# Two-by-two block products in the feed-forward input of a decoder layer

## The chip, the cores and the metric

The kernel runs on one core of a Trainium2 chip. The core has TensorE (matrix products, PE in the profile, its weight loads PEld), VectorE (DVE), ScalarE (ACT), GpSimd (POOL) and SyncE (SP, which here only issues transfers). Each engine works through its own list of instructions in order and waits on semaphores for the others. The metric is device time in microseconds (us) for one execution. Times from a profile are those of one profiled execution.

## The reference

The program is one layer of a decoder for 256 tokens of width 1024: gated attention and a recurrent branch, cross attention to a memory, and a feed-forward part. Only the last one is touched by the change:

```python
hn = rmsnorm(h, norm_ffn_g[l])
gu = hn @ w_ffn_in[l]
h = h + (jax.nn.silu(gu[..., :FFN_HIDDEN]) * gu[..., FFN_HIDDEN:]) @ w_ffn_out[l]
return rmsnorm(h, final_norm_g)
```

FFN_HIDDEN is 2816. So w_ffn_in is 1024 by 5632 and w_ffn_out 2816 by 1024, all in float32. rmsnorm divides each token by its root mean square and multiplies by a gain per feature.

## The kernel before, in words

A float32 product is made of three products of a shorter format: each operand is split into a part "hi" (the value rounded to the short format) and "lo" (the remainder), and hi by hi, hi by lo and lo by hi are summed in PSUM (mm3t, L237).

All weights come in units of 128 x 2048 values (1 MB), in the order of the list ORDER, one transfer each. prep (L169) sends one unit for, lets ScalarE copy it to hi (L194, two pieces of 1024 columns), and lets VectorE (576 columns of each piece) and GpSimd (448 of each piece) subtract to get lo (L198). There are two buffers for raw units and three pairs of hi and lo; nxt (L205) keeps two units of lead. The order of TensorE's instructions is as written in the code; on the other engines a scheduler orders them by the written order and by what is ready.

The feed-forward has eleven groups j of 256 hidden units. A group's input weights are two units ("I", j, kh): kh is the half of the 1024 input features, and the 512 columns are 256 gate columns and 256 value columns. Its output weights are one unit ("O", j). The steps, with the lines of before:

- turn_h2 (L1059) transposes 128 tokens by 512 features of the residual on TensorE, multiplies by the gain on VectorE and splits into H2 on ScalarE and GpSimd. The root mean square of a token is not applied here: it is a factor of a whole row and is applied in the gate.
- ffn_in (L1104) multiplies one unit with 128 tokens: four blocks of 128 features, three matmuls each, 12 matmuls of 512 columns into the bank psi. A group takes 48.
- gate (L1086) makes silu of one half on ScalarE (fg) and multiplies with the other half on VectorE (fu).
- turn_hid (L1094) transposes the gated hidden values (hidT) and splits them.
- ffn_out (L1119) multiplies one output unit: 24 matmuls into four PSUM banks acc, which stay open over the whole feed-forward.

The loop (L1125) goes I(j,0), turn_hid(j-1), I(j,1), O(j-1); the last output units are woven into the tail. PSUM has four banks for psi and hidT (pool mm) and four for acc.

In the attention's output product before it (pso), the residual H is updated and the first three of the four turn_h2 stand between its parts.

## Time and profile before

| | us |
|---|---|
| median of 3 runs | 624.67 (624.52 to 625.46) |
| the profiled execution | 625.08 |
| its span, first to last instruction | 623.1 |
| TensorE busy | 615.1 |
| VectorE busy | 395.6 |
| ScalarE busy | 334.1 |
| GpSimd busy | 371.5 |

The feed-forward's first matmul starts at 431.1 us. A row of the timeline gives start, length, engine, line, operation, output<-input and count; rows of a window table give, after the window, the busy time of PE, PEld, DVE, ACT and POOL with their counts, the granted TensorE clock, the share of the transfer engines and GB/s. A row of a group gives count, then busy time and mean nanoseconds, then the idle time ahead of it and what ended that.

### The profile page before, as it was taken

The numbers are of one execution on the slowest core, as the hardware profiler recorded it, in microseconds if no ns is written. First come the engines' busy times: TensorE is split into PE (matmuls) and PEld (weight loads), VectorE is DVE, ScalarE is ACT, GpSimd is POOL, SyncE is SP. The second block draws the span as 40 slices with busy tenths as digits, with TensorE's granted clock in tenths as the row PEclk, the third lists the DMA queues.
The fourth block names the chain that finished last, engine by engine and source line by source line (L and its number), as shares of the span: only waits on it lengthen the run. The fifth ranks groups of instructions, "written<-read, shape, count | busy, mean of one in ns | idle before, by whom it ended". The sixth has DMA issues, their size and how long they took to land.

```text
span 623.1 us, 8546 instructions
## 1 busy us (share of the span) xinstructions
PE 615.1 (99%) x3153; PEld 513.7 (82%) x3153; DVE 395.6 (63%) x691; ACT 334.1 (54%) x550; POOL 371.5 (60%) x296
## 2 busy tenths in 40 slices
PE   8999999999999999999999999999999999999995
PEld 7888888888877877778888888888888888888884
DVE  7589888979776875748846456754444444444433
ACT  7785554234376866727547556644543344434432
POOL 3888744556544564356857876656655665566553
PEclk9999999999999999999999999999999999999999
DMA  8754553334433333545454544453354455455511
GB/s 346 288 197 149 203 202 136 136 135 147 191 137 135 136 136 136 203 174 191 145 213 189 187 176 178 143 196 135 136 180 175 187 202 184 177 184 198 204 68 68
DMA packets 16890, 107.53 MB, mean 173 GB/s; under 512 B 2000, under 2 KB 2640, under 8 KB 4560
## 3 DMA queue, kind: packets, MB, share of 16 engines
q1 hardware_dynamic: 16128, 106.14, 46.9%
q10 hardware_dynamic: 720, 0.84, 0.4%
q8 instruction: 25, 0.41, 0.3%
q14 instruction: 17, 0.14, 0.1%
HBM read 105.92 MB, written 1.05 MB: 172 GB/s over the span
## 4 chain that ended last, share of the span: by engine, by line
PE 98%; DVE 0%; POOL 0%; issue 0%; POOLq 0%; DVEq 0%
PE pst L238 13%; PE pst L240 13%; PE pst L239 13%; PE psf L259 7%; PE psi L238 6%; PE psi L240 6%; PE psi L239 6%; PE psf L260 4%; PE acc L240 3%; PE acc L238 3%; PE acc L239 3%; PE lp L613 2%; PE psg L514 1%; PE pso L238 1%; PE pso L240 1%; PE pso L239 1%
## 5 line engine op out<-in xcount | busy, mean ns | idle before, releaser
L198 POOL TENSOR_TENSOR lo<-raw,hi 128x448 fp32r<-128x448 f32 x172 | 272.0, 1597 | 181.4 <-ACT hi L194 178.4
L194 ACT ACTIVATE hi<-raw 128x1024 fp32r<-128x1024 f32 (+1 forms) x194 | 196.2, 1037 | 161.1 <-PE pst L240 58.2
L198 DVE TENSOR_TENSOR lo<-raw,hi 128x576 fp32r<-128x576 f32 (+2 forms) x194 | 197.8, 1024 | 127.9 <-ACT hi L194 126.1
L238 PE MATMUL pst<-hi,XX 128*128 128x512 f32 x224 | 90.4, 404 | 0.0
L240 PE MATMUL pst<-hi,XX 128*128 128x512 f32 x224 | 87.4, 390 | 0.0
L239 PE MATMUL pst<-lo,XX 128*128 128x512 f32 x224 | 87.3, 390 | 0.0
L238 PE MATMUL psi<-hi,H 128*128 128x512 f32 x176 | 69.6, 395 | 0.0
L240 PE MATMUL psi<-hi,H 128*128 128x512 f32 x176 | 68.7, 390 | 0.0
L239 PE MATMUL psi<-lo,H 128*128 128x512 f32 x176 | 68.5, 389 | 0.0
L240 PEld LDWEIGHTS pst<-hi,XX 128*128 128x128 f32 x224 | 42.0, 188 | 9.0
L238 PEld LDWEIGHTS pst<-hi,XX 128*128 128x128 f32 x224 | 42.1, 188 | 8.8 <-issue 0.7
L239 PEld LDWEIGHTS pst<-lo,XX 128*128 128x128 f32 x224 | 42.1, 188 | 7.9
L240 PEld LDWEIGHTS psi<-hi,H 128*128 128x128 f32 x176 | 33.0, 188 | 7.1
L239 PEld LDWEIGHTS psi<-lo,H 128*128 128x128 f32 x176 | 33.1, 188 | 6.6
L238 PEld LDWEIGHTS psi<-hi,H 128*128 128x128 f32 x176 | 33.1, 188 | 6.5
L238 PE MATMUL acc<-hi,hid 128*128 128x512 f32 x86 | 33.6, 390 | 0.0
L240 PE MATMUL acc<-hi,hid 128*128 128x512 f32 x86 | 33.5, 389 | 0.0
L239 PE MATMUL acc<-lo,hid 128*128 128x512 f32 x86 | 33.5, 389 | 0.0
L1091 DVE SCALAR_TENSOR_TENSOR fu<-psi,r_h,fg 128x256 f32<-128x256 f32 x22 | 10.6, 483 | 25.1 <-ACT fg L1089 25.1
L1089 ACT ACTIVATE fg<-psi,r_h 128x256 f32<-128x256 f32 x22 | 10.4, 475 | 29.1 <-PE psi L240 29.1
L259 PE MATMUL psf<-H,hi 128*128 128x512 f32 x64 | 22.8, 400 | 0.0
L259 PE MATMUL psf<-XX,hi 128*128 128x512 f32 x64 | 22.6, 396 | 0.0
(336 smaller groups left out, 1199.4 us busy)
## 6 DMA issues: line engine op xcount, KB each, us to landing
raw<-w SPq DMA_DIRECT2D x94, 1024.0 KB, 4.8
raw<-w SPq DMA_DIRECT2D x4, 512.0 KB, 6.5
raw<-w SPq DMA_DIRECT2D x4, 256.0 KB, 4.0
H<-xtok SPq DMA_DIRECT2D x1, 1024.0 KB, 9.6
mraw<-mT SPq DMA_DIRECT2D x1, 1024.0 KB, 4.9
xraw<-xT SPq DMA_DIRECT2D x1, 512.0 KB, 6.5
gfin<-gfin SPq DMA_DIRECT2D x1, 512.0 KB, 3.7
out<-H SPq DMA_DIRECT2D x2, 256.0 KB, 2.0
```

Of the source, the lines that this page charges most:

```text
L194: SC.activation(hi[:, a], raw[:, a], AF.Copy)
L198: eng.tensor_tensor(lo[:, b], raw[:, b], hi[:, b].bitcast(F32), op=ALU.subtract)
L238: PE.matmul(ps, xh, h, start=first, stop=False)
L239: PE.matmul(ps, xh, l, start=False, stop=False)
L240: PE.matmul(ps, xl, h, start=False, stop=last)
L259: PE.matmul(ps, w[0][:, k, a], X2[:, :, k], start=k == 0, stop=False)
L260: PE.matmul(ps[:, 0], w[1][:, k, a], X2[:, 0, k], start=False, stop=k == 7)
L514: PE.matmul(pss[c][t], z[:, k, t * 128:(t + 1) * 128], ws[c][0][:, k], start=z is Xh and k == 0, stop=False)
L613: PE.matmul(ps[:, j], KS[:, a0 + j], QQ[:, a0 + j], start=True, stop=True)
L1089: SC.activation(g, ps[:, 0:256], AF.Silu, scale=r)
L1091: V.scalar_tensor_tensor(u, ps[:, 256:512], r, g, op0=ALU.mult, op1=ALU.mult)
```

## The change

Six of the eleven groups are joined to three double groups, (2,3), (5,6) and (8,9). In a double group the tokens are two halves, the features two halves and the weights four units: block 11 is I(q,0), 21 is I(q,1), 12 is I(q+1,0), 22 is I(q+1,1). Each output (group by token half) is the sum of two block products, eight in all. Now they are formed from seven products of combined blocks, called P1 to P7: three with plain tokens (P1, P2, P4) and four with sums and differences of token blocks, which token_sums makes once (tile SS). Weight blocks are combined in place on VectorE, two combinations ahead of P6 and two ahead of P5; each of the seven blocks is then split to hi and lo. Four of the products add up in one bank (P1, P6, P5, P3); ScalarE keeps its value after P1, P6 and P5, and VectorE adds a kept value to another bank (whole), after which the gate runs on GpSimd. Groups 0, 1, 4, 7 and 10 stay as they were.

A product is 12 matmuls, as one ffn_in part is. The plan has 42 units to split (10 I, 21 P, 11 O), where there were 33.

With it go: the split in one piece (VectorE 1152 columns, GpSimd 896) from the third unit on; a fourth pair of split tiles (px) and three units of lead; the root mean square applied to H before the transposes (hn), as sums of tokens need it, and no more in the gate; the first three units' parts for the first 128 tokens ahead of the second token half's transposes.

```diff
+SEVEN = ("P1", "P2", "P6", "P7", "P5", "P3", "P4")
+    out = two(0) + two(1)
+    out += seven(2, P2=[0], P5=[1]) + two(4)
+    out += seven(5, P2=[2], P7=[3], P5=[4]) + two(7)
+    out += seven(8, P2=[5], P7=[6], P5=[7])
+    out += [("I", 10, 0), ("O", 8), ("I", 10, 1)]
+    return out + [("O", 9), ("O", 10)]
...
+        def halve(raw, n):
+            if n % 4 == 3:
+                hi, lo = px[:, 0:2048], px[:, 2048:4096]
...
+            pieces = 2 if n < 2 else 1
...
+                SC.activation(hi[:, a], raw[:, a], AF.Copy)
+                cut = (c + 1) * w - POOL_COLS // pieces
+                V.tensor_tensor(lo[:, c * w:cut], raw[:, c * w:cut], hi[:, c * w:cut].bitcast(F32), op=ALU.subtract)
+                G.tensor_tensor(lo[:, cut:a.stop], raw[:, cut:a.stop], hi[:, cut:a.stop].bitcast(F32),
+                                op=ALU.subtract)
...
+        def block(q, name):
...
+                    SY.dma_start(blk[key], A["w"][where[("I",) + c]])
...
+            if name == "P6":
+                V.tensor_tensor(blk["12"], blk["22"], blk["12"], op=ALU.subtract)
+                V.tensor_tensor(blk["11"], blk["12"], blk["11"], op=ALU.add)
+                return blk["11"]
+            if name == "P7":
+                return blk["12"]
+            if name == "P5":
+                V.tensor_tensor(blk["21"], blk["21"], blk["11"], op=ALU.subtract)
+                V.tensor_tensor(blk["11"], blk["22"], blk["11"], op=ALU.subtract)
+                return blk["11"]
+            return blk["22"] if name == "P3" else blk["21"]
...
-        def gate(o, t):
-            r, ps = two["r"][:, t:t + 1], psi.pop((o, t))
-            g = t2("fg", (128, 256))
-            SC.activation(g, ps[:, 0:256], AF.Silu, scale=r)
-            u = t2b("fu", (128, 256))
-            V.scalar_tensor_tensor(u, ps[:, 256:512], r, g, op0=ALU.mult, op1=ALU.mult)
+        def gate(o, t, eng=V):
+            ps = psi.pop((o, t))
+            g = t2b("fg", (128, 256))
+            SC.activation(g, ps[:, 0:256], AF.Silu)
+            u = t2("fu", (128, 256))
+            eng.tensor_tensor(u, ps[:, 256:512], g, op=ALU.mult)
...
+        def token_sums():
+            a11, a12, a21, a22 = (h2g[t, c] for t in range(2) for c in range(2))
+
+            def put(i, g):
+                SC.activation(SS[:, 0, i], g, AF.Copy)
+                G.tensor_tensor(SS[:, 1, i], g, SS[:, 0, i].bitcast(F32), op=ALU.subtract)
+
+            V.tensor_tensor(a22, a21, a22, op=ALU.add)
+            s2 = t2("s2", (128, 4, 128))
+            V.tensor_tensor(s2, a22, a11, op=ALU.subtract)
+            put(1, s2)
+            V.tensor_tensor(a21, a11, a21, op=ALU.subtract)
+            put(2, a21)
+            put(0, a22)
+            V.tensor_tensor(a12, a12, s2, op=ALU.subtract)
+            put(3, a12)
...
+        def keep(key, ps, home):
+            SC.activation(home, ps, AF.Copy)
+            kept[key] = home
+
+        def whole(q, t, ps, key, eng):
+            c = t2("fc")
+            V.tensor_tensor(c, ps, kept.pop(key), op=ALU.add)
+            psi[q, t] = c
+            gate(q, t, eng)
...
+        prep_u(3)
+        for n in range(3):
+            ffn_in(n, 0)
+        turn_h2(1, hn1)
+        ffn_in(0, 1)
+        prep_u(4)
+        token_sums()
+        ffn_in(1, 1)
...
+        for n in range(4, len(units) - 2):
+            prep_u(n + 3)
```

More of the change, by code (lines that the diff above doesn't have):

```diff
@@ L70, with ffn_plan, seven, two @@
 ORDER = plan()
+SEVEN = ("P1", "P2", "P6", "P7", "P5", "P3", "P4")
+def ffn_plan():
+    def seven(q, **after):
+        out = []
+        for p in SEVEN:
+            out.append(("P", q, p))
+            out += [("O", o) for o in after.get(p, ())]
+        return out
+    def two(j):
+        return [("I", j, 0), ("I", j, 1)]
+    out = two(0) + two(1)
[4 more added lines that the diff above has]
+    return out + [("O", 9), ("O", 10)]
+FFN_PLAN = ffn_plan()
 def lay(ws):
@@ L1051, in build @@
         at[0] += 4
-        gfin = big("B4", "gfin", (128, 1024))
+        gf = big("B4", "gf", (128, 2048))
+        gfin = gf[:, 0:1024]
         SY.dma_start(gfin, A["gfin"].to_broadcast([128, 1024]))
@@ L1055, in build @@
         h2h, h2l = H2[:, 0], H2[:, 1]
+        where = {u: i for i, u in enumerate(ORDER)}
+        px = big("P1", "px", (128, 4096), F32R)
+        made_u, pair, blk = [0], {}, {}
+        def halve(raw, n):
+            if n % 4 == 3:
+                hi, lo = px[:, 0:2048], px[:, 2048:4096]
+            else:
+                hi = wh.tile([128, 2048], F32R, name="hi", tag="hi")
+                lo = wl.tile([128, 2048], F32R, name="lo", tag="lo")
+            pieces = 2 if n < 2 else 1
+            w = 2048 // pieces
+            for c in range(pieces):
+                a = slice(c * w, (c + 1) * w)
+                SC.activation(hi[:, a], raw[:, a], AF.Copy)
[3 more added lines that the diff above has]
+                                op=ALU.subtract)
+            return hi, lo
@@ new lines, in block @@
+        def block(q, name):
+            if name == "P1":
+                blk.clear()
+                for key, tag, c in (("11", "B10", (q, 0)), ("21", "B11", (q, 1)),
+                                    ("22", "B12", (q + 1, 1)), ("12", "B6", (q + 1, 0))):
+                    blk[key] = big(tag, "b" + key, (128, 2048))
+                    SY.dma_start(blk[key], A["w"][where[("I",) + c]])
+                return blk["11"]
+            if name == "P2":
+                return blk["21"]
+            if name == "P6":
[7 more added lines that the diff above has]
+                V.tensor_tensor(blk["11"], blk["22"], blk["11"], op=ALU.subtract)
+                return blk["11"]
+            return blk["22"] if name == "P3" else blk["21"]
@@ L1056, in wo_part, with prep_u @@
+        units = FFN_PLAN
+        def prep_u(upto):
+            while made_u[0] <= min(upto, len(units) - 1):
+                n = made_u[0]
+                made_u[0] += 1
+                u = units[n]
+                if u[0] == "P":
+                    raw = block(u[1], u[2])
+                else:
+                    raw = wr.tile([128, 2048], F32, name="raw", tag="raw")
+                    SY.dma_start(raw, A["w"][where[u]])
+                pair[n] = halve(raw, n)
         def wo_part(ps, t, c, kh):
@@ L1057, in wo_part @@
             t_part(ps, wo[2 * c + kh], (oxh, oxl), t, kh)
-        def turn_h2(t, c):
-            ks, ts = slice(4 * c, 4 * c + 4), slice(t * 128, (t + 1) * 128)
-            bk = bank("h2T", (128, 4, 128))
-            for j in range(4):
-                k = 4 * c + j
-                PE.transpose(bk[:, j], H[:, t, k * 128:(k + 1) * 128], ident)
-            g = t2("h2g", (128, 4, 128))
-            V.tensor_tensor(g, bk, bc(gv[:, V_FFN + 4 * c:V_FFN + 4 * c + 4], 128, 2), op=ALU.mult)
-            SC.activation(h2h[:, ks, ts], g, AF.Copy)
-            G.tensor_tensor(h2l[:, ks, ts], g, h2h[:, ks, ts].bitcast(F32), op=ALU.subtract)
@@ L1070, in build, with add_h2, rstd_h2 @@
-        todo = None
+        ssq2 = cp.tile([128, 4], F32, name="ssq2")
+        v2 = cp.tile([128, 2], F32, name="v2")
+        r2 = cp.tile([128, 2], F32, name="r2")
+        h2g = {}
+        def add_h2(t, c, ps):
+            d = H[:, t, c * 512:(c + 1) * 512]
+            V.tensor_tensor(d, ps, d, op=ALU.add)
+            SC.activation(t2b("hjunk"), d, AF.Square, scale=1.0 / 32.0, accum_out=ssq2[:, 2 * t + c:2 * t + c + 1])
+        def rstd_h2(t):
+            V.tensor_scalar(v2[:, t:t + 1], ssq2[:, 2 * t:2 * t + 1], ssq2[:, 2 * t + 1:2 * t + 2], EPS,
+                            op0=ALU.add, op1=ALU.add)
+            G.tensor_tensor(r2[:, t:t + 1], v2[:, t:t + 1], nhalf[:, :1], op=ALU.pow)
+            hn = []
+            for c in range(2):
+                n = t2("hn")
+                SC.activation(n, H[:, t, c * 512:(c + 1) * 512], AF.Copy, scale=r2[:, t:t + 1])
+                hn.append(n)
+            return hn
@@ new lines, in turn_h2 @@
+        def turn_h2(t, hn):
+            for c in range(2):
+                ks, ts = slice(4 * c, 4 * c + 4), slice(t * 128, (t + 1) * 128)
+                bk = bank("h2T", (128, 4, 128))
+                for j in range(4):
+                    PE.transpose(bk[:, j], hn[c][:, j * 128:(j + 1) * 128], ident)
+                g = t2("h2g", (128, 4, 128))
+                V.tensor_tensor(g, bk, bc(gv[:, V_FFN + 4 * c:V_FFN + 4 * c + 4], 128, 2), op=ALU.mult)
+                SC.activation(h2h[:, ks, ts], g, AF.Copy)
+                G.tensor_tensor(h2l[:, ks, ts], g, h2h[:, ks, ts].bitcast(F32), op=ALU.subtract)
+                h2g[t, c] = g
@@ L1071, in build @@
+        hn0 = None
         for t in range(2):
@@ L1074, in build @@
                 wo_part(ps, t, c, 0)
-                if todo:
-                    turn_h2(*todo)
+                if (t, c) == (1, 1):
+                    turn_h2(0, hn0)
                 wo_part(ps, t, c, 1)
-                add_h(t, c, ps, None, ssq2)
-                todo = (t, c)
-        ring = ("B7", "B14", "B10", "B11", "B12", "B6")
-        X2 = (h2h, h2l)
-        hid, acc, two, psi, hm = {}, {}, {}, {}, {}
-        def gate(o, t):
-            r, ps = two["r"][:, t:t + 1], psi.pop((o, t))
-            g = t2("fg", (128, 256))
-            SC.activation(g, ps[:, 0:256], AF.Silu, scale=r)
-            u = t2b("fu", (128, 256))
-            V.scalar_tensor_tensor(u, ps[:, 256:512], r, g, op0=ALU.mult, op1=ALU.mult)
+                add_h2(t, c, ps)
+            if t == 0:
+                hn0 = rstd_h2(0)
+        hn1 = rstd_h2(1)
+        hids = [big(tag, "hids", (128, 2, 2, 2, 256), F32R) for tag in ("B7", "B14")]
+        X2 = (h2h, h2l)
+        hid, acc, psi, hm = {}, {}, {}, {}
+        def gate(o, t, eng=V):
[4 more added lines that the diff above has]
+            eng.tensor_tensor(u, ps[:, 256:512], g, op=ALU.mult)
             hm[o, t] = u
@@ L1099, in turn_hid @@
                     PE.transpose(bk[:, j, t * 128:(t + 1) * 128], u[:, j * 128:(j + 1) * 128], ident)
-            hd = big(ring[o % 6], "hid", (128, 2, 2, 256), F32R)
+            hd = hids[o // 2 % 2][:, o % 2]
             split(bk, hd[:, 0], hd[:, 1])
             hid[o] = hd
-        def ffn_in(o, kh, t, w):
-            if kh == 0:
-                psi[o, t] = mm.tile([128, 512], F32, name="psi", tag="mm")
-            t_part(psi[o, t], w, X2, t, kh)
         def out_part(o, w, t, c, home=None, u=0, v=512):
@@ L1117, in out_part, with ffn_in @@
                      (o == 0 or home is not None) and k == 0, k == 1 and o >= NF // 2 - (2 if t and c else 1))
-        def ffn_out(o):
-            w = by_k(nxt(), 2)
+        def ffn_in(n, t):
+            _, o, kh = units[n]
+            if kh == 0:
+                psi[o, t] = mm.tile([128, 512], F32, name="psi", tag="mm")
+            t_part(psi[o, t], by_k(pair[n], 4), X2, t, kh)
+            if kh == 1:
+                gate(o, t)
+        SS = big("P0", "SS", (128, 2, 4, 4, 128), F32R)
@@ new lines, in tokens, with product @@
+        def tokens(name):
+            if name in ("P1", "P2", "P4"):
+                t, kh = {"P1": (0, 0), "P2": (0, 1), "P4": (1, 1)}[name]
+                return [[z[:, 4 * kh + k, t * 128:(t + 1) * 128] for k in range(4)] for z in X2]
+            i = {"P5": 0, "P6": 1, "P7": 2, "P3": 3}[name]
+            return [[SS[:, z, i, k] for k in range(4)] for z in range(2)]
+        def product(ps, name, w, first):
+            xh, xl = tokens(name)
+            for k in range(4):
+                for i, (x, z) in enumerate(((xh, w[0]), (xh, w[1]), (xl, w[0]))):
+                    PE.matmul(ps, x[k], z[:, k], start=first and k == 0 and i == 0, stop=k == 3 and i == 2,
+                              skip_group_check=not first)
@@ new lines, in build, with ffn_product @@
+        bank_of, kept = {}, {}
+        def keep(key, ps, home):
[6 more added lines that the diff above has]
+            gate(q, t, eng)
+        def ffn_product(n):
+            _, q, name = units[n]
+            w = by_k(pair[n], 4)
+            key = {"P1": "A", "P6": "A", "P5": "A", "P3": "A", "P2": "B", "P7": "F", "P4": "F"}[name]
+            first = name in ("P1", "P2", "P7")
+            if first:
+                bank_of[key] = mm.tile([128, 512], F32, name="pq" + key, tag="mm")
+            ps = bank_of[key]
+            product(ps, name, w, first)
+            if name == "P1":
+                keep("1", ps, t2("f1"))
+            elif name == "P2":
+                whole(q, 0, ps, "1", G)
+            elif name == "P6":
+                keep("2", ps, gf[:, 1024:1536])
+            elif name == "P5":
+                keep("4", ps, gf[:, 1536:2048])
+                whole(q + 1, 1, bank_of["F"], "4", G)
+            elif name == "P3":
+                psi[q + 1, 0] = ps
+                gate(q + 1, 0)
+            elif name == "P4":
+                whole(q, 1, ps, "2", G)
@@ L1121, in ffn_out @@
+        def ffn_out(n):
+            w = by_k(pair[n], 2)
             for t in range(2):
                 for c in range(2):
-                    out_part(o, w, t, c)
-        for u in ORDER[at[0]:-2]:
-            if u[0] == "O":
-                ffn_out(u[1])
-                continue
-            _, o, kh = u
-            w = by_k(nxt(), 4)
-            for t in range(2):
-                ffn_in(o, kh, t, w)
-                if (o, kh, t) == (0, 0, 0):
-                    turn_h2(1, 1)
-                    two["r"] = rstd2(ssq2, "h2")
-                if kh == 1:
-                    gate(o, t)
-            if kh == 0 and o:
-                turn_hid(o - 1)
+                    out_part(units[n][1], w, t, c)
@@ new lines, in build @@
+        prep_u(3)
[6 more added lines that the diff above has]
+        ffn_in(1, 1)
+        prep_u(5)
+        ffn_in(2, 1)
+        turn_hid(0)
+        prep_u(6)
+        for t in range(2):
+            ffn_in(3, t)
+        to_turn = [1]
+        for n in range(4, len(units) - 2):
+            prep_u(n + 3)
+            u = units[n]
+            if u[0] == "I":
+                for t in range(2):
+                    ffn_in(n, t)
+            elif u[0] == "P":
+                ffn_product(n)
+            else:
+                ffn_out(n)
+            if u[0] != "O" and u[2] in (0, "P1"):
+                for o in to_turn:
+                    turn_hid(o)
+                to_turn = []
+            if u[0] == "I" and u[2] == 1:
+                to_turn = [u[1]]
+            elif u[0] == "P" and u[2] == "P4":
+                to_turn = [u[1], u[1] + 1]
@@ L1143, in build @@
         n = NF // 2 - 1
-        wa = by_k(nxt(), 2)
-        wb = by_k(nxt(), 2)
+        wa, wb = (by_k(pair[len(units) - 2 + i], 2) for i in range(2))
         out_part(n - 1, wa, 0, 0)
@@ L1159, in build @@
         ssq3 = cp.tile([128, 5], F32, name="ssq3")
-        hg3 = {i: big(ring[j], "hg3", (128, 512)) for j, i in enumerate(((0, 0), (0, 1), (1, 0)))}
+        hg3 = {i: big(tag, "hg3", (128, 512)) for tag, i in zip(("B10", "B11", "B12"), ((0, 0), (0, 1), (1, 0)))}
         v3 = cp.tile([128, 3], F32, name="v3")
```

## The prediction

> **What bounds the kernel now.** I read the page first: engines, then the slices, then the costliest groups.

> ```profile
> PE 615.1 (99%) x3153; PEld 513.7 (82%) x3153; DVE 395.6 (63%) x691; ACT 334.1 (54%) x550; POOL 371.5 (60%) x296
> L198 POOL TENSOR_TENSOR lo<-raw,hi 128x448 fp32r<-128x448 f32 x172 | 272.0, 1597 | 181.4 <-ACT hi L194 178.4
> ```

> TensorE is busy throughout and never waits after the first microseconds, so fewer matmuls mean less time as long as it still never waits. The matmul "mean ns" of 390 overlaps its neighbours; what one costs is the distance of two starts. From the timeline of TensorE, then the table by stage for one feed-forward turn (two input units, one output unit) and for the whole feed-forward, and the chain:

> ```profile
> 595.72 0.39 PE L238 MATMUL psi<-hi,H 128*128 128x512 f32 x1
> ...
> 598.89 0.39 PE L240 MATMUL psi<-hi,H 128*128 128x512 f32 x1
> 447.90:464.70 16.80, 16.80 (x77) 13.90 (x76) 7.68 (x9) 7.35 (x9) 10.03 (x6) 1.00 0.53 188
> 430.00:600.00 170.00, 170.00 (x772) 140.73 (x771) 76.14 (x91) 74.52 (x93) 101.77 (x63) 1.00 0.50 181
> 448.10 0.44 PE hidT L1099 x4
> 464.89 0.44 PE hidT L1099 x4
> ```

> The two rows of the fence's top are 14 matmuls apart: 3.17 / 14 = 0.226 us a matmul. Twelve (one block product) take 2.72 us, a unit of 24 takes 5.44 us, and a turn of 72 with its transposes (0.47) the 16.79 us between the two hidT rows. In that turn GpSimd is busy 10.0 us and VectorE 7.7, for three weight units to split. That is slack now; the change splits a weight block per 2.72 us of TensorE, so the question is what a split costs.

> **What a split costs.** One unit's split in the timeline of VectorE and GpSimd, then a turn in which another VectorE instruction came between:

> ```profile
> 477.44 0.76 DVE L198 TENSOR_TENSOR lo<-raw,hi 128x576 fp32r<-128x576 f32 x1 [2.74 <-ACT hi L194]
> 478.39 1.43 DVE L198 TENSOR_TENSOR lo<-raw,hi 128x576 fp32r<-128x576 f32 x1 [0.19 <-ACT hi L194]
> 477.48 3.35 POOL L198 TENSOR_TENSOR lo<-raw,hi 128x448 fp32r<-128x448 f32 x2 [1.77 <-ACT hi L194]
> 466.74 0.69 DVE L286 TENSOR_TENSOR hid<-hidT,hid 128x512 fp32r<-128x512 f32 x1
> 467.50 0.96 DVE L198 TENSOR_TENSOR lo<-raw,hi 128x576 fp32r<-128x576 f32 x1
> 466.11 3.37 POOL L198 TENSOR_TENSOR lo<-raw,hi 128x448 fp32r<-128x448 f32 x2 [2.09 <-ACT hi L194]
> 476.34 2.01 ACT L194 ACTIVATE hi<-raw 128x1024 fp32r<-128x1024 f32 x2 [3.12 <-PE acc L240]
> ```

> The same VectorE instruction takes 0.76 us when it starts first and 1.43 when it starts in the middle of GpSimd's. It ends at 479.82; GpSimd's first of two pieces ends at the half of 3.35, at 479.16, and 0.66 us is left. So it stood still until GpSimd's instruction was over, and GpSimd's second piece then stood still for it: 4 turns, 0.66 + 1.01 + 0.66 + 1.01 = 3.35. An instruction of VectorE that reads two SBUF tiles and one of GpSimd exclude each other for their whole length. The hid row (one operand in PSUM) ran at its usual 0.69 beside GpSimd. I treat both engines' two-tile work as one queue, "the shared queue". Prices in it:

> ```profile
> L198 DVE TENSOR_TENSOR lo<-raw,hi 128x1024 fp32r<-128x1024 f32 x14 | 18.1, 1316 | 3.8 <-ACT hi L194 3.8
> 14.13 1.22 DVE L198 TENSOR_TENSOR lo<-raw,hi 128x1024 fp32r<-128x1024 f32 x1
> L198 DVE TENSOR_TENSOR lo<-raw,hi 128x512 fp32r<-128x512 f32 x8 | 5.4, 694 | 0.6 <-ACT hi L194 0.6
> 418.23 1.29 POOL L1068 TENSOR_TENSOR H<-h2g,H 128x512 fp32r<-128x512 f32 x1 [5.57 <-ACT H L1067]
> 387.02 0.74 POOL L973 TENSOR_TENSOR qxl<-kx,qxh 128x256 fp32r<-128x256 f32 x1 [1.82 <-ACT qxh L972]
> ```

> The new split is one piece each, 1152 and 896 columns: twice the pieces above less one fixed part (0.06), 1.27 + 1.96 = 3.23 us. A 2048-column combination is 2.2 (two of 1.22, each less some 0.1 of start). 512 columns cost 0.6 on VectorE and 1.17 on GpSimd, 256 on GpSimd 0.62: the rows less the 0.1 that lies outside the exclusion (0.76 against 0.66).

> **The change, part by part.** All sums are against the profiled execution (625.08 us, span 623.1); the median of the runs is 624.67, 0.4 lower.

> Matmuls: seven products of 12 instead of eight, three times: 36 x 0.2264 = 8.15 us less on the path. Transposes keep their number. That is the whole gain.

> Splits: 42 units (10 plain input, 21 products, 11 output) instead of 33. TensorE needs 63 x 2.72 + 11 x 0.47 = 176 us for them; the shared queue 42 x 3.23 = 136, 12 combinations 26, nine 256-column gate products now on GpSimd 6, token sums (4 of 0.6, 4 of 1.17) 7, the token transposes' two late remainders 2: 177. They are equal, so TensorE waits wherever the work bunches. I followed the changed program's engine queues, which are in order, with these prices.

> Transfers are the same megabytes. On SP's queue the four blocks of a group now wait for splits of the group before, and hold the next units behind them; landing takes 4.8 us (row below) and the nearest user comes some 10 us after the issue, so I cost this at nothing. What is queued behind a late block is VectorE's first combination, and behind that the gate that frees P3's bank: 4 us of slack.

> ```profile
> raw<-w SPq DMA_DIRECT2D x94, 1024.0 KB, 4.8
> L1066 DVE TENSOR_TENSOR h2g<-h2T,gv 128x512 f32<-128x512 f32 x4 | 2.8, 688 | 6.2 <-PE h2T L1064 6.2
> L1067 ACT ACTIVATE H<-h2g x4: 617/632/633, 417.5 to 435.2; 128x512 fp32r<-128x512 f32 x4
> ```

> Opening. The normed tokens must be whole before they are summed, so the second half turns only after three parts of 12. Its first psi part then waits for VectorE 0.69, ScalarE 0.63 and GpSimd: 1.9 us of TensorE idle before it. From there the shared queue holds, until the gate of unit (1, second tokens), which turn_hid(1) after P1 needs: two remainders 2.3, four sums 2.4, four sum remainders 4.7, three combinations 6.6, VectorE's part of P1, P2, O0 3.8, GpSimd's of P1, P2, O0, P6 7.8, and the gate 0.4: 28.0. TensorE has 16.8 in that stretch (three parts 8.16, turn 0.47, unit 5.44, P1 2.72). Stall 1.9 + 11.2 = 13.1, spread over the start and the turns of hidden 0 and 1. The floor is 2.6, if nothing excludes; the ceiling 18.7, with the GpSimd rows' 1.67 a piece (waits in them), 1.4 more for four.

> First double group to second. From there to GpSimd's gate product for P4, which turn_hid(2) needs: P6's VectorE part 1.3, eight splits (P7, P5, O1, P3, P4, I, I, P1) 25.8, GpSimd's part of the next P2 2.0, three combinations 6.6, three gates 1.9: 37.6. TensorE has P2, O0, P6, P7, P5, O1, P3, P4, I: 32.6. The stall is 4.6 to 5.0; I take 4.6 as the gate starts a little before. Then P1 waits 1.3 for a PSUM bank whose gate stands on VectorE behind a combination. Sum 5.9.

> Second to third: eleven splits 35.5, P2's two parts 3.2, four combinations 8.8, three gates 1.9: 49.4 against TensorE's 47.6. The bare difference is 1.8; three splits here (O2, P5, P3) come late, as ScalarE's copy (2.0, row above) waits for TensorE to free the pair or stands behind gates, and in my walk the queue is empty for some 3 us by that, of which half is lost. Stall 3.5, and the same 1.3: 4.8. For both later groups the floor is nothing, where the exclusion fails.

> Third to the end: no next group is prepared; O8 waits 1.9 for the hidden split behind O9's. The last output units and the tail are as before.

> Costed at nothing: ScalarE's copies (42 x 2.0 and some 40 small ones of 0.6 are 110 of about 195 us), the fourth pair of split tiles and the longer lead (they only let splits start earlier), the gate without its scale, the norm applied before the turn (four copies of 0.63, hidden by the three parts in front; it is what makes the opening wait).

> Sum: 13.1 + 5.9 + 4.8 + 1.9 - 8.15 = +17.5, so 642.6 as a profiled run and 642 as a median. Longer GpSimd pieces by a seventh (2.23 a block) bring it to 650, shorter by a tenth to 638.

> **The rivals.** *Faster.* The exclusion does not carry over to one long piece, or VectorE and GpSimd overlap; then of the stalls stay 2.6 at the opening and a few tenths, -8.15 + 2.8 = -5.3, 619. It decides where a split costs the shared queue less than about 2.7 us: group one then needs 32.6. Against it stands the 1.43 row, met in each turn I looked at. *Only the opening waits*, as later groups have some slack that I priced too tight: 13.1 - 8.15, 630. For it: between groups two and three the bare sums differ by 1.8 only. *The clock falls in the gaps.* TensorE has never been idle so far except at both ends:

> ```profile
> 1.56 3.57 PE L335 MATMUL warm<-still 128*128 128x256 f32 x15 [1.56 <-DVE still L332]
> 387.01 0.28 PE L238 MATMUL xs<-kxh,qxh 128*128 128x256 f32 x1
> 387.13 0.28 PE L239 MATMUL xs<-kxl,qxh 128*128 128x256 f32 x1
> 618.00:623.00 5.00, 0.00 (x0) 0.00 (x0) 0.91 (x3) 0.72 (x1) 0.55 (x1) 0.80 0.42 157
> ```

> The first fifteen matmuls run at 0.238 us each against 0.12 later, for 3.6 us: a cold start loses 1.8. A mean granted clock of 0.80 over the last 5 us, at half speed 2 of them, has it fall near 621, 4.4 us after the last matmul (about 616.6). My gaps are about 5.0, 3.9, 4.6 and 3.5 us. If all four lose 1.8 the time is 642 + 7 = 649; part is given back where the shared queue is late anyway. [...] *The change does not do what it says* is out: 36 matmuls fewer stand in the program.

> **How the numbers follow.** Main case, 636 to 645: 0.57. Clock as well, 646 to 651: 0.17. Only the opening, 628 to 635: 0.13. Faster, about 619: 0.11. Even, where both halves cancel: 0.02. The range 630 to 650 leaves out the faster case and a little at both ends. 0.2% (1.2 us) is about what a measurement here can tell: faster 0.11, same 0.02, slower 0.87.

> **What the profile would show.** Right: TensorE with some 25 us of idle in the feed-forward, before hidT of hidden 0 and 1, hidT of 2 and 5, released by VectorE or GpSimd gates; VectorE and GpSimd instructions there at two and three times their lone lengths (a split's VectorE part between 1.3 and 3.3, a combination 2.2 to 4.2); about 3117 matmuls. Wrong: splits side by side at 1.3 and 2.0 to 2.1 with TensorE unbroken, or gaps released by transfers. The largest risk is GpSimd's price for 896 columns, which no row shows in one piece.

## The result and the profile after

| | before | changed |
|---|---|---|
| median (us) | 625.07 (624.52 to 625.53) | 645.41 (644.99 to 645.98) |
| profiled execution, span (us) | 625.08, 623.1 | 644.99, 642.9 |

The ratio is 1.0326 (95% interval 1.0309 to 1.0344): the changed kernel is 20.3 us slower. The forecast was 642, range 630 to 650.

The first page of the changed kernel's profile, engines and slices (each digit the busy tenths of 16.1 us, PEclk the granted clock in tenths):

```profile
PE 614.4 (96%) x3117; PEld 510.3 (79%) x3117; DVE 457.5 (71%) x685; ACT 356.7 (55%) x545; POOL 424.7 (66%) x288
PE   8999999999999999999999999998889699799995
POOL 3888643665436643548768676555999879959843
PEclk9999999999999999999999999998899799999998
```

TensorE executes 36 matmuls less (3153 before) and yet is busy almost as long (615.1 before): part of its work, 10.1 us, ran at half clock (0.50 in the windows below). In slices 28 to 35 (434 to 563 us) it has holes, GpSimd is nearly full, and the clock row dips there too. What TensorE waited for in the feed-forward, from the table of waits (line, what it waited for: us in total, times, longest). Here hidT is the bank that turn_hid fills, and "hidden 2" below is its turn for group 2; pqA, pqB and pqF are the banks of the products:

```profile
PE hidT L1207 <- POOL fu L1199: 9.4, 3, 5.7
PE hidT L1207 <- DVE fu L1199: 4.8, 2, 2.5
PE psi L261 <- ACT H L1172: 2.8, 1, 2.8
PE pqA L1261 <- DVE hids L309: 0.9, 1, 0.9
PE acc L263 <- DVE hids L309: 0.8, 1, 0.8
PE psi L263 <- POOL H L1173: 0.8, 2, 0.4
PE acc L261 <- ACT hids L308: 0.5, 1, 0.5
```

20.0 us, 14.2 of them before the hidden turns (hidT) for a gate (fu). Before, there was no such wait at all. The table by stage, for 20 us without a hole in TensorE, and the timeline of GpSimd and VectorE there, show why the gates come late:

```profile
480.00:500.00 20.00, 20.00 (x90) 16.55 (x89) 19.08 (x10) 14.04 (x11) 20.00 (x7) 1.00 0.82 306
484.90 3.25 POOL L1099 TENSOR_TENSOR px<-b,px 128x896 fp32r<-128x896 f32 x1
488.11 3.25 POOL L1099 TENSOR_TENSOR lo<-b,hi 128x896 fp32r<-128x896 f32 x1
491.31 3.24 POOL L1099 TENSOR_TENSOR lo<-raw,hi 128x896 fp32r<-128x896 f32 x1
494.52 2.78 POOL L1199 TENSOR_TENSOR fu<-fc,fg 128x256 f32<-128x256 f32 x1
486.08 3.28 DVE L1098 TENSOR_TENSOR lo<-b,hi 128x1152 fp32r<-128x1152 f32 x1
489.89 2.67 DVE L1098 TENSOR_TENSOR lo<-raw,hi 128x1152 fp32r<-128x1152 f32 x1
493.11 3.60 DVE L1115 TENSOR_TENSOR b<-b,b 128x2048 f32<-128x2048 f32 x1 [0.54 <-DMA b<-w]
505.68 2.77 POOL L1199 TENSOR_TENSOR fu<-fc,fg 128x256 f32<-128x256 f32 x1
508.50 1.54 PE L1207 MATMUL hidT<-cst,fu 128*128 128x128 f32 x6 [5.66 <-POOL fu L1199]
```

GpSimd is busy for 20.00 of 20.00 us and starts a split every 3.21 us (484.90, 488.11, 491.31). A split must come every 2.72 us where TensorE runs one product after the other. VectorE's part of a split, 1.27 alone by the forecast, lies between 2.67 and 3.28 in these rows, and GpSimd's product of 256 columns takes 2.78, of which 0.62 was the forecast price alone: each stands still inside its row until the other engine's instruction is over (the VectorE row at 486.08 ends at 489.36, 1.21 us behind the end of GpSimd's row at 484.90). The lateness piles up until the gate that hidden 2 needs is over at 508.45, and TensorE has stood for 5.66 us.

### The profile page after: what moved, and what is told of

Same layout as the page of the kernel before. It is cut to its first block, busy times and chain, and to the rows that moved or that the text cites. A ratio compares the mean times of both kernels' runs of the same rounds, so it can differ in the third digit from the quotient of the medians.

```text
span 642.9 us, 8467 instructions
## 1 busy us (share of the span) xinstructions
PE 614.4 (96%) x3117; PEld 510.3 (79%) x3117; DVE 457.5 (71%) x685; ACT 356.7 (55%) x545; POOL 424.7 (66%) x288
## 4 chain that ended last, share of the span: by engine, by line
PE 75%; DVE 8%; POOL 6%; issue 4%; DMA 4%; ACT 3%; POOLq 0%; DVEq 0%; ACTq 0%
PE pst L261 13%; PE pst L263 12%; PE pst L262 12%; PE psf L282 7%; PE psf L283 4%; DVE lo L1098 3%; POOL lo L1099 3%; ACT hi L1096 2%; POOL px L1099 2%; PE pqA L1261 2%; PE lp L636 2%; DMA raw<-w 2%; PE acc L263 2%; DMA b<-w 1%; PE acc L261 1%
## 5 line engine op out<-in xcount | busy, mean ns | idle before, releaser
L221 POOL TENSOR_TENSOR lo<-raw,hi 128x448 fp32r<-128x448 f32 x106 | 161.9, 1541 | 111.4 <-ACT hi L217 108.5
L217 ACT ACTIVATE hi<-raw 128x1024 fp32r<-128x1024 f32 (+1 forms) x128 | 128.7, 1028 | 93.9 <-PE pst L263 58.1
L221 DVE TENSOR_TENSOR lo<-raw,hi 128x576 fp32r<-128x576 f32 (+2 forms) x128 | 130.1, 1024 | 58.3 <-ACT hi L217 57.1
L1099 POOL TENSOR_TENSOR lo<-raw,hi 128x896 fp32r<-128x896 f32 (+1 forms) x21 | 60.8, 2900 | 7.1 <-ACT hi L1096 6.0
L1099 POOL TENSOR_TENSOR lo<-b,hi 128x896 fp32r<-128x896 f32 x13 | 42.3, 3252 | 15.8 <-ACT hi L1096 13.8
L1098 DVE TENSOR_TENSOR lo<-raw,hi 128x1152 fp32r<-128x1152 f32 (+1 forms) x21 | 37.1, 1769 | 16.7 <-ACT hi L1096 16.6
L1096 ACT ACTIVATE hi<-raw 128x2048 fp32r<-128x2048 f32 (+1 forms) x21 | 36.5, 1748 | 11.7 <-DMA raw<-w 4.1
L263 PE MATMUL acc<-hi,hids 128*128 128x512 f32 x86 | 33.6, 391 | 0.8 <-DVE hids L309 0.8
L261 PE MATMUL acc<-hi,hids 128*128 128x512 f32 x86 | 33.7, 392 | 0.5 <-ACT hids L308 0.5
L261 PE MATMUL psi<-hi,H 128*128 128x512 f32 x64 | 26.3, 410 | 2.8 <-ACT H L1172 2.8
L1099 POOL TENSOR_TENSOR px<-b,px 128x896 fp32r<-128x896 f32 x8 | 27.6, 3449 | 1.4 <-ACT px L1096 1.3
L263 PE MATMUL psi<-hi,H 128*128 128x512 f32 x64 | 26.1, 407 | 0.8 <-POOL H L1173 0.8
L262 PE MATMUL psi<-lo,H 128*128 128x512 f32 x64 | 25.9, 405 | 0.0
## 6 DMA issues: line engine op xcount, KB each, us to landing
raw<-w SPq DMA_DIRECT2D x82, 1024.0 KB, 4.8
b<-w SPq DMA_DIRECT2D x12, 1024.0 KB, 5.4
H<-xtok SPq DMA_DIRECT2D x1, 1024.0 KB, 9.2
mraw<-mT SPq DMA_DIRECT2D x1, 1024.0 KB, 4.9
```

The costliest lines, as they stand in the source:

```text
L217: SC.activation(hi[:, a], raw[:, a], AF.Copy)
L221: eng.tensor_tensor(lo[:, b], raw[:, b], hi[:, b].bitcast(F32), op=ALU.subtract)
L261: PE.matmul(ps, xh, h, start=first, stop=False)
L262: PE.matmul(ps, xh, l, start=False, stop=False)
L263: PE.matmul(ps, xl, h, start=False, stop=last)
L1096: SC.activation(hi[:, a], raw[:, a], AF.Copy)
```

## The experiments

Two questions: is it the exclusion of VectorE and GpSimd (the shared queue) that costs the time, or the placing of the products, or the opening? And what does the clock add? In e1, e2 and e8 only the split of the 42 feed-forward units changes.

**e1: VectorE splits alone.**

```diff
+FFN_POOL = 0
-                cut = (c + 1) * w - POOL_COLS // pieces
+                cut = (c + 1) * w - FFN_POOL // pieces
```

GpSimd's instruction stands only where cut leaves it columns.

> The changed kernel, but VectorE makes the remainders of all 2048 columns in the feed-forward and GpSimd none (42 splits at 2.2 us on VectorE instead of 1.27 + 1.96). Shared queue (VectorE's two-tile work and GpSimd's exclude each other): 1.0 us less per split, 42 us less in that queue; the wait before the turn of hidden 2 falls from 5.7 to under 2, the one before hidden 5 goes, and about half of the opening's stays. 626 to 630 in all, GpSimd's lengths near their lone values. Rival, VectorE overloaded on its own (its 457 us busy are its own work, GpSimd is beside it): 0.9 us more per split on VectorE, the same waits or longer, 645 to 655. Rival, only the number of splits and the order of the lists matter: no change, 643 to 647.

Measured: 629.93 (629.31 to 630.04), ratio 1.0073 (1.0058 to 1.0088). A group of splits, then the waits:

```profile
L1099 DVE TENSOR_TENSOR lo<-b,hi 128x2048 fp32r<-128x2048 f32 x13 | 31.6, 2429 | 10.2 <-ACT hi L1097 10.2
PE hidT L1209 <- DVE fu L1201: 2.1, 1, 2.1
PE hidT L1209 <- POOL fu L1201: 1.7, 1, 1.7
```

One engine alone does all 2048 columns in 2.43 us, where two engines together needed 3.21. Giving one engine 44% of the columns made the pair slower than the other engine by itself. The waits before hidT fall from 14.2 to 3.8 us, and three quarters of the loss are gone (15.5 of 20.3 us).

**e2: half of GpSimd's share** (FFN_POOL = 448).

> The changed kernel with GpSimd's share of a feed-forward split halved, 448 of 2048 columns (VectorE 1600). Shared queue: a split costs 1.73 + 1.02 = 2.75 instead of 3.23, so the time lies between that of the change and that of the kernel without GpSimd's share, 629 to 634, and most of the gain is here already, as 2.75 is about what fits beside TensorE. Rival, the two engines overlap and the longer of both lists decides: VectorE 0.5 us longer a split, 645 to 650.

Measured: 633.85 (632.73 to 634.49), ratio 1.0132 (1.0115 to 1.0148), waits before hidT 6.5 us. By GpSimd's columns the time goes 629.9 (0), 633.9 (448), 645.4 (896): the second half costs three times the first, as one would expect of a queue that has some slack first and then none.

**e8: GpSimd as long at work, but only writing.** Two fills of its 896 columns take the place of the subtraction. It leaves out 7/16 of the remainders.

```diff
-                G.tensor_tensor(lo[:, cut:a.stop], raw[:, cut:a.stop], hi[:, cut:a.stop].bitcast(F32),
-                                op=ALU.subtract)
+                for _ in range(2):
+                    G.memset(lo[:, cut:a.stop].bitcast(F32), 0.0)
```

> The changed kernel; in place of its subtraction GpSimd fills its 896 columns of each feed-forward remainder with zeros, twice (so 7 of 16 of the weights' remainders are left out there). GpSimd keeps an instruction per split but reads no tile. If it is the reading of tiles by both that excludes: VectorE's parts stand at 1.3 us and its combinations at 2.2, the waits go as with VectorE alone, 620 to 630. If any instruction of GpSimd keeps VectorE out: VectorE's parts still at 2 to 3 us, and the time falls only by what the fill is shorter than the subtraction, 632 to 645.

Measured: 623.27 (622.66 to 623.43), ratio 0.9962 (0.9949 to 0.9975). From its timeline, a split of VectorE with GpSimd's fills:

```profile
486.35 1.36 DVE L1098 TENSOR_TENSOR lo<-raw,hi 128x1152 fp32r<-128x1152 f32 x1 [0.84 <-ACT hi L1096]
486.81 1.75 POOL L1100 MEMSET px<- 128x896 f32 x2 [0.96 <-PE pqA L1261]
```

The two run side by side at their lone lengths (1.36 is the length of a VectorE part that nothing disturbs). The eight VectorE parts that go from a block to px last 1.35 us in the mean here and 2.61 to 3.27 in the changed kernel, and the waits before hidT are down to one of 1.5 us. GpSimd is busy 1.75 us a unit, not far from the 1.96 that I had priced for its subtraction. So it is not that GpSimd works, and not that it writes; of what the runs varied, what is left is that both instructions read SBUF. VectorE's sum fc, with one input in PSUM, took 0.68 us beside GpSimd's subtraction in the changed kernel (at 489.29, in GpSimd's row at 488.11), and 0.68 to 0.69 in all six such sums. One thing this run does not hold constant: a fill needs no copy from ScalarE and so starts earlier. The lengths of the VectorE rows do not depend on that.

**e4: the gates on VectorE.** The product behind `whole` (three places) goes from GpSimd's full list to VectorE's.

```diff
-                whole(q, 0, ps, "1", G)
+                whole(q, 0, ps, "1", V)
```

> The changed kernel with the nine gate products on VectorE instead of GpSimd. The longest waits (hidden 2 and 5) ended with such a product on GpSimd. Shared queue: the product only moves to another place in the same queue, behind the same splits and combinations; 256 columns cost 0.33 instead of 0.62: 643 to 647. Rival, the product's place on GpSimd is the cause: 9.4 us of waits go, 635 to 638.

Measured: 649.61 (647.22 to 650.01), ratio 1.0382 (1.0362 to 1.0401); 2.6 us above the range that I expected, and the rival is out.

```profile
PE hidT L1207 <- DVE fu L1199: 15.5, 4, 5.5
```

The list in which the gate stands does not matter: its product waits for the same queue, now behind splits and combinations on VectorE. The waits in the feed-forward together are 20.3 us, as in the changed kernel; what the trace has more of is slow matmuls, 16.6 us of them at half clock (in three stretches of 6.83 us) against 10.1. No run separates the two.

**e10: the order alone.** The double groups are (3,4), (6,7) and (8,9), with other output units between them; GpSimd's share stays at 896.

```diff
-    out = two(0) + two(1)
-    out += seven(2, P2=[0], P5=[1]) + two(4)
-    out += seven(5, P2=[2], P7=[3], P5=[4]) + two(7)
+    out = two(0) + two(1) + [("I", 2, 0), ("O", 0), ("I", 2, 1)]
+    out += seven(3, P2=[1], P5=[2]) + two(5)
+    out += seven(6, P2=[3], P7=[4])
     out += seven(8, P2=[5], P7=[6], P5=[7])
-    out += [("I", 10, 0), ("O", 8), ("I", 10, 1)]
+    out += two(10) + [("O", 8)]
...
-            if u[0] != "O" and u[2] in (0, "P1"):
+            if u[0] != "O" and u[2] in (0, "P2" if u[1] == 8 else "P1"):
```

> The changed kernel with its splits and gates as they are (GpSimd 896 columns), and only the order of the kernel e9: the third plain group ahead of the first double group, the output units of e9. Shared queue: the opening's waits shrink, but each later group still asks 37 and more us of the queue in 33 of TensorE, so the work only meets later: 637 to 643. Rival, the crowded opening and the order are what cost the time and the share of GpSimd little: 624 to 630.

Measured: 643.82 (642.31 to 647.69), ratio 1.0313 (1.028 to 1.0347), 0.8 us above the range that I expected; its rival is out. The interval overlaps that of the changed kernel (1.0309 to 1.0344).

```profile
PE hidT L1207 <- POOL fu L1199: 12.3, 3, 6.4
PE pqF L1261 <- DVE fc L1272: 2.7, 1, 2.7
```

The waits move to other hidden turns and stay nearly as large (18.9 us in all for 20.0). With the queue full, spreading its work helps little or nothing.

**e3: the frame without products.** All units plain, no token sums; the norm ahead of the turn, the new opening and the one-piece splits stay.

```diff
-    out += seven(2, P2=[0], P5=[1]) + two(4)
-    out += seven(5, P2=[2], P7=[3], P5=[4]) + two(7)
-    out += seven(8, P2=[5], P7=[6], P5=[7])
+    for j in range(2, 10):
+        out += two(j) + [("O", j - 2)]
...
-        token_sums()
```

> The changed kernel's frame without its products: all eleven groups as plain units (33 splits), no token sums; the norm before the transposes, three parts for the first tokens ahead of the second turn, the fourth pair and the one-piece split stay. It has the matmuls of the kernel before. Shared queue: 33 x 3.23 = 107 us beside 180 of TensorE, so no wait but the opening's 1.9 + 0.8 before the first part for the second tokens: 627 to 629. Rival, the opening as such (new order, late norm) costs the 13 us that were put down to it: 636 to 640.

Measured: 630.78 (628.45 to 631.55), ratio 1.0082 (1.0061 to 1.0102), 2 us above what I expected. Its only waits in the feed-forward are those for the turned tokens:

```profile
PE psi L260 <- ACT H L1171: 2.2, 1, 2.2
PE psi L262 <- POOL H L1172: 1.0, 2, 0.6
```

That is 3.2 us; 3.4 us at half clock behind them (445.4 to 448.8, TensorE running throughout) lose 1.7 more. So the opening as such costs some 5 of the 5.7 us, and with 33 units to split, even in one piece each, no gate is late.

**e7: matmuls into two of the gaps**, to keep the clock up. 20 ahead of hidT of hidden 2 and 12 ahead of hidden 5, into a bank that is overwritten.

```diff
+            flat = bk.rearrange("p a b -> p (a b)")
+            for _ in range({2: 20, 5: 12}.get(o, 0)):
+                PE.matmul(flat, h2h[:, 0, 0:128], px[:, 0:512], start=True, stop=True)
```

> The changed kernel with matmuls whose result is overwritten ahead of the transposes of hidden 2 (20) and hidden 5 (12), 4.5 and 2.7 us of work in gaps of 5.7 and 3.5. The granted clock should stay full after the first of these gaps (it was half for 6.8 us from 505.3 on). If the half clock costs its full price, 3 us come back: 641 to 643. If the shared queue is late there anyway, TensorE only waits longer at the next turn (hidden 5): 644 to 646.

Measured: 645.48 (644.61 to 645.98), ratio 1.032 (1.0303 to 1.0338): nothing changed. Around hidden 2 the clock is full now, but in this run it is halved around hidden 1 (rows by windows: start:end, length, busy PE, PEld, DVE, ACT, POOL, clock, transfers):

```profile
505.30:512.10 6.80, 6.80 (x36) 5.67 (x35) 6.70 (x3) 2.92 (x3) 6.80 (x3) 1.00 0.08 34
465.09:468.50 3.41, 0.44 (x2) 0.20 (x2) 3.41 (x1) 0.52 (x1) 3.41 (x2) 1.00 0.21 29
468.50:471.91 3.41, 2.69 (x8) 2.21 (x9) 3.41 (x3) 1.96 (x2) 2.28 (x1) 0.50 0.67 279
```

TensorE ran for 9.5 us at half speed, with a third window from 444.6 on, against 10.1 in the changed kernel, so the run does not measure the clock's price. It is its rival (644 to 646) that came in. What the run does show: filling a gap shortens nothing when the gate is late for another reason. The waits fall to 12.9 us, and the 32 added matmuls are 32 x 0.2264 = 7.2: 20.1 again.

**b1: the kernel before with VectorE alone** splitting in the feed-forward, as a control.

```diff
+FFN_FIRST = ORDER.index(("I", 0, 0))
-                cut = (c + 1) * n - (0 if i in ALONE else POOL_COLS // pieces)
+                cut = (c + 1) * n - (0 if i in ALONE or i >= FFN_FIRST else POOL_COLS // pieces)
```

> The kernel before with VectorE making all of the remainders in the feed-forward, as a control: nothing waits for splits there (a 16.8 us turn has 10 us of them), so no change on either theory, 624.5 to 626; if the split by VectorE alone were faster in itself, the time would fall here too.

Measured: 625.17, ratio 1.0003 (0.9993 to 1.0012). The gain of e1 is not a gain that the kernel before could have had too: there the queue had slack.

**e9: VectorE alone and the order of e10 together**, splits in two pieces, the gates on VectorE.

```diff
+FFN_POOL = 0
-            pieces = 2 if n < 2 else 1
+            pieces = 2
...
-                whole(q, 0, ps, "1", G)
+                whole(q, 0, ps, "1", V)
```

The other two gates and the order of e10 likewise.

> The changed kernel with splits and gate products on VectorE alone (two pieces), and the double groups at (3,4), (6,7), (8,9) so that a third plain group stands ahead of the first one; output units placed after P2, P7 and P5, and O8 after the last input units. Shared queue: 7 of the 25 us of waits stood in the opening because token sums, three combinations and four splits met there; with 10.9 us more of TensorE's work ahead of them they go. Left are the wait for the second turn (1.9) and two or three of about 1 us: 8.15 - 5 = 3 less than before, 621 to 624. Rival, seven products cannot be fed in this kernel in any order: 628 to 632 as with VectorE's splits alone.

Measured: 622.54 (622.27 to 623.21), ratio 0.9958 (0.9943 to 0.9973): 0.4% faster than before, little but clear of the noise.

```profile
PE hidT L1209 <- DVE fu L1201: 1.6, 1, 1.6
PE psi L264 <- POOL H L1175: 1.0, 2, 0.6
PE psi L262 <- ACT H L1174: 1.0, 1, 1.0
PE pqA L1263 <- ACT gf L1269: 0.7, 1, 0.7
```

Against e1 that is 7.4 us for three edits at once (order, pieces, gates), which I did not take apart. What differs from e10 is that the same order stands here on a queue with slack; that this is why it pays is argued, not shown.

**e11: e9 with the opening's late work moved.** One more part for the first tokens ahead of the second turn's use, and the token sums behind hidden 0's turn.

```diff
         turn_h2(1, hn1)
+        ffn_in(3, 0)
         ffn_in(0, 1)
...
-        token_sums()
+        token_sums()
-        for t in range(2):
-            ffn_in(3, t)
+        ffn_in(3, 1)
```

The second token_sums stands after turn_hid(0).

> The kernel e9 with one more part for the first tokens (unit (1,1)) between the second turn's transposes and the first part that needs them, and the token sums written after the turn of hidden 0. The wait for the second turn (1.1 + 0.8 in e9) is covered by 2.7 us of matmuls, that before hidden 0 (1.6) goes; about 1 us stays at the turn of hidden 1. 619 to 621. If these waits only move to the next turn: 622 to 623.

Measured: 620.71 (620.04 to 621.37), ratio 0.9933 (0.9921 to 0.9946), 4.3 us faster than before and the best of all.

```profile
PE hidT L1209 <- DVE fu L1201: 1.5, 1, 1.5
PE pqA L1263 <- ACT gf L1269: 0.7, 1, 0.7
PE psi L264 <- POOL H L1175: 0.4, 1, 0.4
```

2.6 us of waits are left of 20.0. By the waits alone the 8.15 us of matmuls should give 5.5; the stretch from the feed-forward's first matmul to the last of the tail, 185.2 us before, is 4.5 shorter. Counted like this, with what half clock costs taken in, between one and two and a half microseconds stay unplaced in e1, e8, e9 and e11.

## Why the prediction was right, and where it was not

**The gain.** 36 matmuls less is what the trace counts. A product of 12 still takes 2.72 us where nothing is late.

**The price of a split** was called the largest risk, as no row showed GpSimd's 896 columns in one piece: 3.23 was forecast for the split, 3.21 is measured where the queue is full, and the shortest of GpSimd's 896-column rows (2.07 us) is the forecast 1.96 and the 0.1 that lies outside the exclusion. This step carries the forecast, and e1, e2 and e8 show its mechanism, not only its size.

**The stalls**, start-to-start gaps of TensorE less one pitch of 0.23:

| | predicted | measured | places |
|---|---|---|---|
| opening | 13.1 | 9.4 | before psi 0.5, 2.8, 0.8, 0.4; hidden 0: 2.35; hidden 1: 2.55 |
| first to second double group | 5.9 | 6.0 | hidden 2: 5.7; psi 0.35 |
| second to third | 4.8 | 4.5 | hidden 5: 3.5; pqA 1.0 |
| end | 1.9 | 1.9 | 0.3, 0.6, 1.0 |
| sum | 25.7 | 21.9 | |

The 0.8, the 0.4 and the 0.35 stand at half clock, where one pitch is 0.43 (445.48 to 445.91): 0.2 of each is slow matmul and no stall.

How full the shared queue was can be counted from the rows of the trace (VectorE instructions with two SBUF inputs and GpSimd's, overlaps once). From the first part for the second tokens (443.54) to the turn of hidden 1 (469.53) it was occupied 25.9 of 26.0 us; to the turn of hidden 2 (508.50) 38.9 of 39.0; to hidden 5 (561.59) 49.2 of 53.1, with one empty piece of 3.9. The forecast had 28.0, 37.6, and 49.4 with some 3 empty. So the mechanism is right in each stretch. The step that was mis-sized is the opening: 28.0 us of queue were put against 16.8 of TensorE, 2 too many. Which of its terms was too large stays open. The stall after the wait before psi came as 4.9 in place of 11.2 for two more reasons: 0.8 us of the waits before psi fall into this stretch, and TensorE itself took 3.2 us longer in it, at half clock.

The empty piece is forecast too, and for its reason, a ScalarE copy that stands behind gates (it starts at 516.96, after two that wait for TensorE):

```profile
518.94 3.31 POOL L1099 TENSOR_TENSOR lo<-b,hi 128x896 fp32r<-128x896 f32 x1 [7.33 <-ACT hi L1096]
```

In the second and third rows of the table the sums are near, their parts less so: 5.7 for 4.6 at hidden 2, 3.5 for 3.5 at hidden 5, and the 1.3 us that P1 waits for a PSUM bank behind a combination came once instead of twice, as the 1.0 at 568.80. What stood behind the combination there was the split of a hidden turn (hids), not a gate.

**The clock** was a rival with 0.17 and no term of the sum. It came in part. The table by windows of the changed kernel, columns as under e7:

```profile
440.49:443.90 3.41, 0.66 (x5) 0.35 (x3) 1.62 (x3) 2.31 (x4) 0.34 (x1) 1.00 1.02 430
443.90:447.31 3.41, 3.00 (x8) 1.94 (x7) 1.21 (x2) 0.68 (x2) 2.16 (x2) 0.50 0.86 360
454.14:457.55 3.41, 1.10 (x7) 0.87 (x7) 3.41 (x4) 1.34 (x2) 3.41 (x3) 1.00 0.01 2
457.55:460.97 3.42, 3.42 (x10) 2.65 (x9) 3.42 (x2) 1.57 (x2) 3.42 (x1) 0.50 0.00 0
501.93:505.34 3.41, 0.92 (x6) 0.51 (x4) 2.02 (x2) 2.22 (x2) 3.41 (x2) 1.00 0.70 279
505.34:508.75 3.41, 0.25 (x1) 0.25 (x2) 3.41 (x2) 0.00 (x0) 3.41 (x3) 0.50 0.00 0
508.75:512.17 3.42, 3.42 (x12) 2.94 (x12) 3.31 (x2) 1.20 (x2) 2.86 (x1) 0.50 0.00 0
556.54:559.95 3.41, 1.56 (x8) 1.04 (x7) 3.41 (x3) 2.30 (x2) 3.41 (x2) 1.00 0.36 151
559.95:563.37 3.42, 1.78 (x11) 1.61 (x12) 3.32 (x3) 1.09 (x2) 3.42 (x2) 1.00 0.00 0
```

TensorE worked 3.00 + 3.42 + 0.25 + 3.42 = 10.1 us at half clock and lost 5.0 by it. With the 0.6 that would count twice left out of the table, the sum is -8.15 + 21.3 + 5.0 = 18.2, against 19.6 measured (the same stretch is 204.9 us long now); 1.4 stay unplaced. So the forecast's 17.5 had its stalls 4.4 us too large and the clock 5.0 too small, and that the total fits is partly luck. The two are not independent. 3.3 of the 5.0 were lost up to hidden 2, where the queue was hardly ever empty (0.2 us of 65): matmuls at full clock would then have waited longer instead, as the prediction said of a queue that is late anyway. This is worked out from the trace; no run holds the clock full throughout. A step that failed is the fall "4.4 us after the last matmul", read from a single row at the end of the trace: taken as a threshold, it leaves the clock full after the gaps of 2.8 and 2.35 us, and it was 0.50 behind both (from 443.90 and from 457.55), while it stayed at 1.00 behind those of 2.55 and 3.5.

**Costed at nothing.** The hidden turns wait for a gate on VectorE or GpSimd, not for ScalarE. Transfers hold little, but not nothing, and here a term failed: the prediction had the nearest user of a block some 10 us after its transfer was issued. VectorE's first combinations waited 0.54 us (the row at 493.11) and 3.1 us for a block. The chain of work that ended last has that transfer issued at 541.20, when GpSimd's split has freed the buffer, and its user stands ready 1.8 us later:

```profile
541.20 4.78 DMA b<-w
546.08 2.54 DVE L1115 TENSOR_TENSOR b<-b,b 128x2048 f32<-128x2048 f32 x1 [3.09 <-DMA b<-w]
```

GpSimd used the queue in that time, so what this wait cost TensorE was not isolated. It goes with the full queue: in e1 no combination waits for a block, in e8 one does, for 0.51 us. Near the end the chain runs through a transfer again:

```profile
601.59 3.30 POOL lo L1099
604.91 4.85 DMA raw<-w
609.84 1.92 ACT hi L1096
```

GpSimd's late split frees a raw buffer late, and the next unit lands behind it; by this chain it is a cause of the 1.9 us at the end as well, beside the order in which I had put the hidden split behind O9's.

**The rivals.** "Faster" (619) fell because the exclusion holds for long pieces as it did for short ones (the 2.61 to 3.27 us above); e8, where GpSimd fills in place of subtracting, lands at 623. "Only the opening" (630) fell with the 5.7 and 3.5 us at hidden 2 and 5.

## What to carry to other kernels

In this kernel a VectorE instruction with two SBUF inputs and a GpSimd instruction that reads SBUF had to be priced as one queue (VectorE's parts into px took 2.61 to 3.27 us beside a subtraction, 1.35 beside a fill). Hold the sum of their lone lengths per unit against TensorE's time per unit (3.23, measured 3.21, against 2.72 here): here it was larger, TensorE ended up waiting (20.0 us), and VectorE alone (2.43 here) was the faster way. Where the queue had slack, as in b1, it made no difference (ratio 1.0003). A change that saves matmuls by adding work that feeds them is worth its gain only where the feeding engines have slack in that very stage; first take the work off the full queue (e1: 15.5 us), and only then move it about (e10: 1.6 us by itself, which its interval does not tell from nothing). And a gap in TensorE of a few microseconds can have a second price in the clock behind it (5.0 us here, worked out from the windows).

## What the runs showed of the hardware that was not expected

```profile
440.39:443.80 3.41, 1.78 (x11) 1.06 (x9) 1.29 (x2) 1.23 (x2) 1.70 (x2) 1.00 1.01 428
443.80:447.21 3.41, 3.41 (x10) 2.65 (x9) 2.53 (x4) 1.26 (x2) 1.94 (x2) 0.50 0.61 255
```

```profile
439.25:442.66 3.41, 2.08 (x13) 1.28 (x11) 1.29 (x2) 1.23 (x2) 1.03 (x1) 1.00 1.03 435
442.66:446.07 3.41, 3.11 (x14) 2.57 (x15) 1.85 (x3) 1.06 (x2) 1.93 (x3) 1.00 1.02 430
```

1.63 us idle in e1's window halves the next, 1.33 in e9's does not. In the feed-forward of the traces read this way the border lies near half a window: the least idle that was followed by half clock is 1.63 us (e1, e8; 1.67 in e3), the most that was not is 1.85 (the changed kernel), so between 1.6 and 1.9 both outcomes are found, and the ends of matmuls are modelled. To come back, a window had to be fuller: the one from 443.90 above was idle for 0.41 us and the clock was full after it, the one from 468.50 in e7 for 0.72 and the next was still at half speed. This was read from the traces afterwards; no run was made to test it alone.
